# Second half of the residual in a hybrid decoder trunk: its sums of squares and its rows made on VectorE and ScalarE instead of by transposes on TensorE

## The chip, the cores and the metric

The kernel runs on one core of one Trainium2 chip. The metric is the device time of one execution in microseconds (us). Lower is better.

## The reference

The reference is one layer of a decoder trunk over 1024 tokens with 1024 channels, all in 32-bit floats. The part around the change is the end of the mixing half and the start of the MLP half:

```python
        m = jax.nn.sigmoid(sa) * y_a + jax.nn.sigmoid(sb) * y_b
        x = x + jnp.einsum("bsd,de->bse", m, w_o[l])      # out projection, residual

        h = rms_norm(x, g_mlp[l])                         # needs the sum of squares of each token
        f = jnp.square(jax.nn.relu(jnp.einsum("bsd,df->bsf", h, w_1[l])))   # up projection, 1024 -> 4096
        x = x + jnp.einsum("bsf,fd->bsd", f, w_2[l])      # down projection, residual
    return rms_norm(x, g_final)
```

`rms_norm` divides each token by the root of the mean of its squares over the channels.

## The kernel before

Every matrix product is done in 32-bit precision from three passes of a reduced form of it: an operand is split into a high part (`...h`) and a low part (`...l`), and the passes are high·high, high·low and low·high. The right operands are split by ScalarE (ACT, high part, L1386) and VectorE (DVE, low part, L1236). Most left operands (weights) are split by two ACT instructions (L65, L67) and one DMA issued from GpSimd (POOL, L66). On top of this, each product of 2 x 2 blocks is done in seven block products instead of eight (a Strassen-Winograd scheme), so sums and differences of blocks stand on DVE: `s1`, `s2`, `s3`, `s4` of the weights (L1695 to L1700) and `gt2` and the like of the tokens.

The order of the instructions on each engine is written out by hand. The lists `gseq` (gate and out projections, and the first two products of the up projection) and `useq` (the rest of the up projection) give the TensorE steps. A step is 12 matmuls of 128x512 on the four operand chunks; the third of each three uses the low part of the weight, the second the low part of the tokens, so the second matmul of a step is the first that needs the low part of the token operand's first half, and the eighth matmul the first that needs the low part of its second half. The tables `GX` and `UX` say what else is done beside each step: `up_load` (a 512 KB weight load from SP), `up_lhs` (the weights' sums and splits), `g_parts` (splits of a token operand), `g_t` (differences of token blocks). A running clock per engine (`clk`, `at`, `later`, `vector_work`) decides between which steps a deferred DVE instruction falls.

The residual `x1[kk, o, c2]` lies with channels on the partitions; `o` is the token half. It is wanted in two forms: normalized, as the token operand of the up projection (`x1_normed`, 8 DVE instructions a half, L482, from `x1`, a vector and the broadcast `rbm` of the reciprocal roots), and as rows of tokens in DRAM (`x1d`), from which the last residual sum reads it much later.

The first half (`o = 0`) takes its sums of squares by ACT squares (`x1_sq`, L1545), DVE adds (`x1_add`) and a column sum of 4 small matmuls (`x1_cols`, tile `cs`, L1574); its rows are turned by 8 DVE transposes (`x1_turn`) and written by 16 DMAs of 128 KB (`x1_rows_out`, L1568). The second half (`o = 1`) goes through `x1_rows`: 32 transposes on TensorE (tile `tr`, L1587), 8 ACT squares that add up along the row as they go (L1592), 8 DVE copies (L1596) and 4 DMAs of 512 KB (L1600). From the sums `x1_root` makes the reciprocal root (tile `stm`), `x1_diag` a diagonal matrix of it (`rdm`, L1627), and `x1_spread` the broadcast (`rbm`, L1637, on TensorE).

The TensorE steps around the change, in order: `go0e` to `go3e` (the last four of the out projection), `gu0a` (first of the up projection, start 905.98 us), the 32 transposes, `gu1a`, `gu2a`, `rbm`, `gu3a`, then `gu0a` to `gu3a` with the second token block, then `f0b`, `f1b`, `f0c`, `f1c`, `f0d`, `f1d`, and so on. The token operand of `f0b` and `f1b` is `gu6h`/`gu6l`; that of the `f0d`, `f1d` steps first `gu7h`/`gu7l` and in their second pass `gu4h`/`gu4l`.

The tiles come from pools. A tile waits until whoever used its slot last is done with it. `T(...)` draws from the pool `acts` (37 slots of 128x1024), which holds residual blocks, raw weights, split operands and rows. Which slot a new `T` gets therefore depends on the whole order of the `T` calls before it. `S(n)` in `up_lhs` draws from a pool of 5 slots for `s1` to `s4`; the first five are taken by `s1`, `s2` of weight pair 0, `s1`, `s2` of pair 1 and `s4` of pair 0, and `s3` of pair 0 is the sixth. Below, `o0_6` is the split of `s2` of pair 0, `o0_4` the split of a block of raw weight `w_1_raw`, and `o2_6` that of `s2` of pair 2, which is made from raw weights `w_4_raw` and `w_5_raw`.

Of the kernel before, what the change touches and what calls it, by code (L numbers as in the profile page):

```python
# [24 lines left out]
EPS = 1e-6  # L25
# [5 lines left out]
def trunk_kernel(ctx: ExitStack, tc: tile.TileContext, x, xt_in, xt_eo, vecs, w_in, w_a_out, w_b_pl, w_b_sq,  # L31
                 w_rg, w_o, w_1, w_2, g_final, out):

    nc = tc.nc
    cp = ctx.enter_context(tc.tile_pool(name="consts", bufs=1))
# [8 lines left out]
    def T(name, dt=F32, shape=(P, S)):  # L44
        return tp.tile(list(shape), dt, tag="T", name=name)
# [8 lines left out]
    HALVES = (slice(0, HS), slice(HS, S))  # L54
# [52 lines left out]
    ident = cp.tile([P, P], F32, name="ident")  # L107
# [371 lines left out]
    def dve(cost, ready, f, *a):  # L479

        fill(ready)
        f(*a)  # L482
        return at("V", cost, ready)
# [441 lines left out]
    def EV(name):  # L925
        return vp.tile([P, HS], F32, tag="ev", name=name)
# [113 lines left out]
    with tc.manual_schedule(engines=ENGINES):  # L1040
# [64 lines left out]
        def bank(name):  # L1105
            return zp.tile([P, HS], F32, tag="z", name=name)
# [430 lines left out]
    rst, rbk = {}, {}  # L1537
# [2 lines left out]

    sqs = []

    def x1_sq(i, m_):
        s = EV(f"sq{i}{m_}")
        nc.scalar.activation(s, x1[i // 2, 0, i % 2][:, HALVES[m_]], AF.Square)  # L1545
        sqs.append((at("A", 0.62, clk["V"]), s))

    def x1_add(n=1):
# [1 line left out]
            ready, s = sqs.pop(1)  # L1550
            later(ready, 0.63, tt, sqs[0][1], sqs[0][1], s, ALU.add)

    def x1_turn(kk):
        for th in range(2):
            r = T(f"x1r{kk}{th}")
            for c2 in range(2):
                src = x1[kk, 0, c2].rearrange("p (m h b j) -> p h m b j", m=2, h=2, j=32)[:, th]
                dst = r.rearrange("p (b m j) -> p m b j", m=4, j=32)[:, 2 * c2:2 * c2 + 2]
                dve(0.65, 0, nc.vector.transpose, dst, src)
            turned.append((kk, th, r))  # L1560

    turned = []

    def x1_rows_out():
        kk, th, r = turned.pop(0)
# [9 lines left out]
                             start=True, stop=True)  # L1575
        at("P", 0.9)

    def x1_rows(*ts):
        for t in ts:
            o, n = divmod(t, 4)  # L1580
            if n == 0:
                rst[o] = cp.tile([P, 6, 4], F32, tag="st6", name=f"stm{o}", bufs=2)
            rows = T(f"x1r{t}")
            for kk in range(2):
                ps = bank(f"tr{t}{kk}")
                for c in range(4):
                    nc.tensor.transpose(ps[:, c * P:(c + 1) * P],  # L1587
                                        x1[kk, o, c // 2][:, c % 2 * HS + n * P:c % 2 * HS + (n + 1) * P],
                                        ident)
                at("P", 0.45)  # L1590
                a = T(f"sq{t}{kk}")[:, 0:HS]
                nc.scalar.activation(a, ps, AF.Square, accum_out=rst[o][:, kk, n:n + 1])  # L1592
                at("A", 0.63, clk["P"])

                def copy(rows, kk, ps, t):
                    nc.vector.tensor_copy(  # L1596
                        rows[:, HALVES[kk]].rearrange("p (g c j) -> p c g j", g=4, c=4),
                        ps.rearrange("p (c g j) -> p c g j", g=4, c=4))
                    if kk:
                        nc.sync.dma_start(x1d[t], rows)  # L1600

                later(clk["P"], 0.63, copy, rows, kk, ps, t)
            if t == 7:
                x1_root(1)
            if o:
                vector_work(clk["V"])

    def x1_root(o):

        if o == 0:  # L1610
            rst[o] = cp.tile([P, 6, 4], F32, tag="st6", name=f"stm{o}", bufs=2)
        a, b, v, s = (rst[o][:, i, :] for i in range(4))
        if o:
            tt(v, a, b, ALU.add)
        nc.vector.tensor_scalar(v, v if o else sqs[1][:, 0:4], 1.0 / D, EPS, ALU.mult, ALU.add)
        nc.scalar.activation(s, v, AF.Sqrt)
        at("A", 1.5)

# [23 lines left out]
    def x1_normed(kk, o):  # L1642
        for c2 in range(2):
            hq[kk, o, c2] = src = a = x1[kk, o, c2]
            for i in range(2):
                c = 4 * kk + 2 * c2 + i
                dve(0.68, 0, nc.vector.scalar_tensor_tensor, a[:, HALVES[i]], src[:, HALVES[i]],
                    gmlp_c[:, c:c + 1], rbk[o], ALU.mult, ALU.mult)
# [136 lines left out]
    def g_get(n, f):  # L1785
# [57 lines left out]
    with tc.manual_schedule(engines=ENGINES):  # L1843
        for n, step in enumerate(bseq[2:], 2):
            taps["paused"] = False
            clk["A"], clk["V"] = max(clk["A"], clk["P"] + 0.5), max(clk["V"], clk["P"] - 2)
            b_post(*bseq[n - 1])
            b_mm(*step)
            for f, *a in BX.get(step, ()):
                f(*a)  # L1850
            vector_work(clk["P"] - 0.3)
        b_post(*bseq[-1])
        for n in range(len(gseq) + 1):
            clk["A"], clk["V"] = max(clk["A"], clk["P"] + 0.5), max(clk["V"], clk["P"] - 2)
            g_get(n - 1, g_post)
            if n == o0 + 22:
                x1_root(0)
            if n > o0:
                vector_work(clk["V"])
                if n == u0:  # L1860
                    to_mlp()
            g_get(n + 3, g_gate)
            g_get(n, g_mm)
            g_get(n + 4, g_lhs)
            g_get(n + 5, g_sums)
            for f, *a in GX.get(n, ()):
                f(*a)
            vector_work(clk["P"] - 0.3)
# [428 lines left out]
```

## Time and profile before

| | |
|---|---|
| time, median of 3 runs | 1528.98 us (1528.98 to 1529.56) |
| the profiled execution's own time | 1529.02 us |
| its span in the trace | 1527.2 us |
| mean granted TensorE clock | 0.998 |
| TensorE busy | 1517.7 us (99%) |
| VectorE busy | 1200.8 us (79%) |
| ScalarE busy | 927.0 us (61%) |
| GpSimd busy | 192.3 us (13%) |

The span runs from the first to the last instruction; the time has 1.8 us around it. In the lines of the profile a start and a duration are in us; a row "x4" is four instructions that follow each other; "[3.37 <-PE f0c]" is idle time before the row and what ended it. Neighbouring rows overlap a little, so the pitch of instructions (from start to start) is shorter than the duration of one.

### The profile page before, as it was taken

What the parts mean: (1) busy time and instruction counts of PE and PEld (TensorE: products, weight loads), DVE (VectorE), ACT (ScalarE), POOL (GpSimd) and SP (SyncE); (2) the same over time, 40 slices, a digit from 0 to 9 for tenths busy, and PEclk for the clock granted to TensorE, in tenths of its full rate; (3) what the DMA queues carried; (4) which work ended last, traced back from release to release, by engine and by line L of the source; (5) the groups of instructions that cost most, each with busy time, mean ns of one, the idle gap of its engine ahead of it and who ended that gap; (6) DMA issues with size and microseconds to landing.
All of it is one profiled execution on the core that took longest, in us unless ns stands there. A gap on an engine that the chain in (4) does not pass through costs nothing.

```text
span 1527.2 us, 18954 instructions
## 1 busy us (share of the span) xinstructions
PE 1517.7 (99%) x6712; PEld 1249.8 (82%) x6712; DVE 1200.8 (79%) x1640; ACT 927.0 (61%) x1299; POOL 192.3 (13%) x228
## 2 busy tenths in 40 slices
PE   9999999999999999999999999999999999999998
PEld 7878887888888888888888888888888888888886
DVE  7899996999999997788869879755555387777777
ACT  6749688586566657645575777554444455545475
POOL 0111011022222222000022322000000000101010
PEclk9999999999999999999999999999999999999999
DMA  9756778698997789863779897333333974776465
GB/s 352 187 145 159 176 177 191 193 260 213 266 260 173 186 207 273 292 231 121 263 205 302 186 200 189 124 126 111 111 111 111 307 261 129 187 201 167 110 123 153
DMA packets 130943, 295.48 MB, mean 193 GB/s; under 512 B 12912, under 2 KB 34928, under 8 KB 130848
## 3 DMA queue, kind: packets, MB, share of 16 engines
q1 hardware_dynamic: 98816, 214.60, 41.1%
q0 software_dynamic: 31600, 79.15, 28.2%
q8 instruction: 52, 0.85, 0.2%
q10 hardware_dynamic: 432, 0.53, 0.1%
q14 instruction: 43, 0.35, 0.1%
HBM read 148.74 MB, written 60.82 MB: 137 GB/s over the span
## 4 chain that ended last, share of the span: by engine, by line
PE 98%; DMA 1%; DVE 0%; issue 0%; SPq 0%; ACT 0%; DVEq 0%
PE z L745 16%; PE d1b L2017 2%; PE d2b L2017 2%; PE d0b L2017 2%; PE d3b L2017 2%; PE d0e L2017 1%; PE d0a L2017 1%; PE d3e L2017 1%; PE d3a L2017 1%; PE d1e L2017 1%; PE d1a L2017 1%; PE d2e L2017 1%; PE d2a L2017 1%; PE z L274 1%; PE rg L552 1%; PE rg L554 1%
## 5 line engine op out<-in xcount | busy, mean ns | idle before, releaser
L745 PE MATMUL z<-xh,win_h 128*128 128x512 f32 x368 | 115.5, 391 | 0.0
L745 PE MATMUL z<-xl,win_h 128*128 128x512 f32 x368 | 115.0, 390 | 0.0
L657 DVE SCALAR_TENSOR_TENSOR y<-u,vec,y 128x511 f32<-128x511 f32 (+14 forms) x120 | 88.2, 735 | 0.0
L745 PE MATMUL z<-xh,win_l 128*128 128x512 f32 x368 | 87.5, 390 | 0.0
L657 DVE SCALAR_TENSOR_TENSOR yt<-u,vec,yt 128x511 f32<-128x511 f32 (+6 forms) x112 | 82.4, 736 | 0.0
L657 DVE SCALAR_TENSOR_TENSOR y<-yt,csum,y 128x511 f32<-128x511 f32 (+6 forms) x112 | 82.4, 736 | 0.0
L745 PEld LDWEIGHTS z<-xh,win_h 128*128 128x128 f32 x368 | 69.1, 188 | 15.9 <-ACT win_h L67 0.5
L745 PEld LDWEIGHTS z<-xl,win_h 128*128 128x128 f32 x368 | 69.1, 188 | 14.9
L745 PEld LDWEIGHTS z<-xh,win_l 128*128 128x128 f32 x368 | 69.1, 188 | 14.6
L562 ACT ACTIVATE g<-rg,vec 96x1024 f32<-96x1024 f32 x32 | 35.5, 1110 | 72.9 <-PE rg L554 72.9
L1712 ACT ACTIVATE o<-s 128x512 fp32r<-128x512 f32 x56 | 33.7, 623 | 45.2 <-DVE s L1696 26.4
L66 POOL DMA_DIRECT2D zo<-zw x45 | 39.2, 871 | 134.7 <-ACT zo L65 116.8
L503 DVE SCALAR_TENSOR_TENSOR v<-xb,vec,v 128x1023 f32<-128x1023 f32 (+2 forms) x36 | 46.2, 1282 | 5.8 <-ACT v L494 4.9
L66 POOL DMA_DIRECT2D db_10l<-br x4 | 3.5, 876 | 338.3 <-DMA br<-in_w_dram 253.0
L66 POOL DMA_DIRECT2D win_l<-win_raw x23 | 20.0, 868 | 194.2 <-ACT win_l L65 159.4
L65 ACT ACTIVATE zo<-zw 128x512 fp32r<-128x512 f32 x45 | 28.2, 626 | 24.2 <-PE z2f L946 2.1
L1236 DVE TENSOR_TENSOR o<-s,o 128x512 fp32r<-128x512 f32 x56 | 37.3, 683 | 1.5 <-ACT o L1712 1.5
L66 POOL DMA_DIRECT2D zo<-zs x30 | 26.4, 879 | 74.9 <-ACT zo L65 62.8
L67 ACT ACTIVATE zo<-zw 128x512 fp32r<-128x512 f32 x45 | 27.9, 621 | 0.0
L598 DVE TENSOR_TENSOR_SCAN g<-a,g 128x1024 f32<-128x1024 f32 x12 | 27.5, 2291 | 0.4
L66 POOL DMA_DIRECT2D ga<-gsa x8 | 7.0, 874 | 161.0 <-DMA m<-mbd 150.8
L1236 DVE TENSOR_TENSOR o<-w_raw,o 128x512 fp32r<-128x512 f32 x38 | 25.9, 683 | 0.0
(3178 smaller groups left out, 4910.1 us busy)
## 6 DMA issues: line engine op xcount, KB each, us to landing
w_raw<-in_w_dram SPq DMA_DIRECT2D x32, 512.0 KB, 5.1
br<-in_w_dram SPq DMA_DIRECT2D x32, 512.0 KB, 5.8
ar<-fd SPq DMA_DIRECT2D x32, 512.0 KB, 6.6
zw<-in_w_in_dram SPq DMA_DIRECT2D x28, 512.0 KB, 6.9
win_raw<-in_w_in_dram SPq DMA_DIRECT2D x23, 512.0 KB, 4.6
win_l<-win_raw POOLq DMA_DIRECT2D x23, 512.0 KB, 4.8
zo<-zw POOLq DMA_DIRECT2D x45, 256.0 KB, 5.8
gates<-zg SPq DMA_DIRECT2D x32, 256.0 KB, 4.4
```

Source lines behind the costliest of these rows:

```text
L65: nc.scalar.activation(l, src, AF.Copy, scale=-1.0)
L66: nc.gpsimd.dma_start(l, src, accum_op=ALU.add)
L67: nc.scalar.activation(h, src, AF.Copy)
L274: nc.tensor.matmul(z0[i][:, HALVES[hf]], w0[i][w][:, k, :], xpart(a, hf, k), start=k == 0 and which == "hh", stop=k == 7 and which == ("hl ...
L503: nc.vector.scalar_tensor_tensor(v[:, d:S], a[:, 0:S - d], cbw_c[:, w * 12 + t:w * 12 + t + 1], v[:, d:S], ALU.mult, ALU.add)
L562: nc.scalar.activation(a, gps.pop((n, gi))[:HD, :], AF.Sigmoid, bias=(ba_c, bx_c)[gi][:, n:n + 1])
L598: nc.vector.tensor_tensor_scan(i, a, i, 0.0, ALU.mult, ALU.add)
L657: nc.vector.scalar_tensor_tensor(o[:, k:], a[:, 0:HS - k], c, o[:, k:], ALU.mult, add)
L745: nc.tensor.matmul(zps[s][:, HALVES[hf]], w[:, k, :], xw[k][part][hf], start=n == 0, stop=n == 23)
L1236: tt(l, src, h.bitcast(F32), ALU.subtract)
L1712: nc.scalar.activation(o[:, 0], src, AF.Copy)
L2017: nc.tensor.matmul(o, a, b, start=start and n == 0, stop=stop and n == len(todo) - 1, skip_group_check=not start or not stop)
```

## The change

The second half goes the first half's way. Eight ACT squares and seven DVE adds are put among the last steps of the out projection (`o0+24` to `u0+0`), the column sum of 4 small matmuls stands where the transposes stood, behind `gu0a`, and `x1_root(1)` is called one step later, at `u0+1`. `up_lhs(0, 6)` moves from `u0+0` to `u0+1`. `x1_normed` of the second half writes four new `T` tiles (`hq`) instead of overwriting `x1`, because the rows are now turned later, by 8 DVE transposes in the `useq` steps 12 to 18 and written by 16 DMAs of 128 KB in the steps 14 to 20. The 16 row DMAs of the first half move up from the `useq` steps 8 to 14 of the table to stand right behind their transposes. `x1_rows` is gone.

```diff
-    def x1_sq(i, m_):
-        s = EV(f"sq{i}{m_}")
-        nc.scalar.activation(s, x1[i // 2, 0, i % 2][:, HALVES[m_]], AF.Square)
+    def x1_sq(i, m_, o=0):
+        if o and (i, m_) == (0, 1):
+            sqs.clear()
+        name = f"sq{i}{m_}{o}"
+        s = T(name)[:, 0:HS] if o and (i, m_) in ((0, 1), (3, 0)) else EV(name)
+        nc.scalar.activation(s, x1[i // 2, o, i % 2][:, HALVES[m_]], AF.Square)
         sqs.append((at("A", 0.62, clk["V"]), s))
...
-    def x1_turn(kk):
-        for th in range(2):
-            r = T(f"x1r{kk}{th}")
...
     turned = []
+
+    def x1_turn(kk, th, o):
+        r = T(f"x1r{kk}{th}{o}")
+        for c2 in range(2):
+            src = x1[kk, o, c2].rearrange("p (m h b j) -> p h m b j", m=2, h=2, j=32)[:, th]
+            dst = r.rearrange("p (b m j) -> p m b j", m=4, j=32)[:, 2 * c2:2 * c2 + 2]
+            dve(0.65, 0, nc.vector.transpose, dst, src)
+        turned.append((kk, 2 * o + th, r))
...
-    def x1_rows(*ts):
...
     def x1_root(o):
 
-        if o == 0:
-            rst[o] = cp.tile([P, 6, 4], F32, tag="st6", name=f"stm{o}", bufs=2)
-        a, b, v, s = (rst[o][:, i, :] for i in range(4))
-        if o:
-            tt(v, a, b, ALU.add)
-        nc.vector.tensor_scalar(v, v if o else sqs[1][:, 0:4], 1.0 / D, EPS, ALU.mult, ALU.add)
+        rst[o] = cp.tile([P, 6, 4], F32, tag="st6", name=f"stm{o}", bufs=2)
+        v, s = rst[o][:, 2, :], rst[o][:, 3, :]
+        nc.vector.tensor_scalar(v, sqs[1][:, 0:4], 1.0 / D, EPS, ALU.mult, ALU.add)
...
             hq[kk, o, c2] = src = a = x1[kk, o, c2]
+            if o:
+                hq[kk, o, c2] = a = T(f"hq{kk}{c2}")
...
-        20: ((x1_add,), (x1_sq, 3, 1), (flush,), (x1_turn, 0)),
-        21: ((x1_add,), (flush,), (x1_cols,), (x1_turn, 1), (up_load, 0, (1,))),
+        20: ((x1_add,), (x1_sq, 3, 1), (flush,), (x1_turn, 0, 0, 0), (x1_turn, 0, 1, 0),
+             (x1_rows_out,), (x1_rows_out,)),
+        21: ((x1_add,), (flush,), (x1_cols,), (x1_turn, 1, 0, 0), (x1_turn, 1, 1, 0),
+             (x1_rows_out,), (x1_rows_out,), (up_load, 0, (1,))),
         22: ((x1_diag, 0), (up_load, 1, (1,))),
-        23: ((x1_spread, 0), (x1_normed, 0, 0)), 24: ((g_parts, "u", 1, 0), (g_parts, "u", 1, 1)),
-        25: ((x1_normed, 1, 0),), 26: ((g_parts, "u", 2, 0),), 27: ((g_parts, "u", 2, 1),)}.items()})
+        23: ((x1_spread, 0), (x1_normed, 0, 0)), 24: ((g_parts, "u", 1, 0), (g_parts, "u", 1, 1), (x1_sq, 0, 1, 1)),
+        25: ((x1_sq, 1, 1, 1), (x1_sq, 2, 1, 1), (x1_add, 2), (x1_normed, 1, 0), (x1_sq, 3, 1, 1)),
+        26: ((x1_add,), (x1_sq, 0, 0, 1), (x1_add,), (g_parts, "u", 2, 0), (x1_sq, 1, 0, 1)),
+        27: ((x1_add,), (x1_sq, 2, 0, 1), (x1_add,))}.items()})
     u0 = 2 * o0
     GX.update({u0 + n: v for n, v in {
-        0: ((up_lhs, 0, 6), (x1_rows, 4, 5, 6, 7)),
-        1: ((x1_diag, 1),), 2: ((x1_spread, 1), (up_lhs, 1, 6)),
+        0: ((x1_sq, 3, 0, 1), (x1_add,), (flush,), (g_parts, "u", 2, 1), (x1_cols,)),
+        1: ((x1_diag, 1), (up_lhs, 0, 6)), 2: ((x1_spread, 1), (up_lhs, 1, 6)),
...
+            elif n == u0 + 1:
+                x1_root(1)
...
-    UX.update({n: ((x1_rows_out,),) for n in range(8, 16, 2)})
+    UX.update({n: UX.get(n, ()) + ((x1_turn, n // 2 % 2, n // 4 - 3, 1),) for n in (12, 14, 16, 18)})
+    UX.update({n: UX.get(n, ()) + ((x1_rows_out,),) for n in (14, 16, 18, 20)})
```

What this does to the order is seen on three engines. On TensorE, behind the step `gu0a`, before the change:

```order
L1442 MATMUL gu0a<-gu1h_7703,gu_1_7696 128x512
L1587 MATMUL tr_7810<-ident,x_7587 128x128 x2
L1587 MATMUL tr_7810<-ident,x_7620 128x128 x2
L1587 MATMUL tr_7817<-ident,x_7654 128x128 x2
L1587 MATMUL tr_7817<-ident,x_7682 128x128 x2
```

Twelve such rows follow up to the step `gu1a`. After the change, at the same place (in the changed kernel L1576 is the column sum):

```order
L1442 MATMUL gu0a<-gu1l_7720,gu_1_7712 128x512
L1442 MATMUL gu0a<-gu1h_7719,gu_1_7712 128x512
L1576 MATMUL cs<-ones,sq_7722 128x1 x4
L1442 MATMUL gu1a<-gu1h_7716,gu_1_7739 128x512
L1442 MATMUL gu1a<-gu1l_7717,gu_1_7739 128x512
```

The column sum reads `sq_7722`, which the last of the seven adds on VectorE completes. On VectorE, from the diagonal `rdm` of the second half to the first split of the token operand `gu6`, before the change (L1695, L1696, L1698 and L1700 make `s1`, `s2`, `s4` and `s3`; the name's first number is the weight pair; the eight L482 rows with `rbm` are `x1_normed`):

```order
L1627 TENSOR_SCALAR rdm_7908<-ident,stm_7808 128x128 x2
L1695 TENSOR_TENSOR s_1_7937<-w_3_raw 128x512
L1696 TENSOR_TENSOR s_1_7938<-s_1_7937,w_2_raw 128x512
L482 SCALAR_TENSOR_TENSOR x_7587<-x_7587,vec,rbm_7932 128x512 x2
L482 SCALAR_TENSOR_TENSOR x_7620<-x_7620,vec,rbm_7932 128x512 x2
L482 SCALAR_TENSOR_TENSOR x_7654<-x_7654,vec,rbm_7932 128x512 x2
L482 SCALAR_TENSOR_TENSOR x_7682<-x_7682,vec,rbm_7932 128x512 x2
L482 TENSOR_TENSOR x_7141<-x_7587,x_7141 128x1024
L482 TENSOR_TENSOR x_7143<-x_7620,x_7143 128x1024
L482 TENSOR_TENSOR gt2u_7988<-x_7654,x_7141 128x1024
L482 TENSOR_TENSOR gt2u_7989<-x_7682,x_7143 128x1024
L1698 TENSOR_TENSOR s_0_8073<-w_0_raw,s_0_7801 128x512
```

After it (L1666, L1667, L1669 and L1671 are the same four):

```order
L1596 TENSOR_SCALAR rdm_7871<-ident,stm_7846 128x128 x2
L1666 TENSOR_TENSOR s_0_7876<-w_1_raw 128x512
L1667 TENSOR_TENSOR s_0_7877<-s_0_7876,w_0_raw 128x512
L1666 TENSOR_TENSOR s_1_7908<-w_3_raw 128x512
L1667 TENSOR_TENSOR s_1_7909<-s_1_7908,w_2_raw 128x512
L1669 TENSOR_TENSOR s_0_8048<-w_0_raw,s_0_7877 128x512
L1671 TENSOR_TENSOR s_0_8050<-w_0_raw,w_1_raw 128x512
L482 SCALAR_TENSOR_TENSOR hq_7935<-x_7595,vec,rbm_7903 128x512 x2
```

The sums of weight pair 0 stood ahead of `rdm` (`s1`, `s2`) and behind the `gt2u` rows (`s4`, `s3`); all four now stand between `rdm` and `x1_normed`. On SP, which issues the loads, the load of `w_5_raw` keeps its place behind the four `fd` stores of the first up projection steps; what it waits for is another. Before:

```order
L1501 DMA fd<-f_2_8040 128x512 [waits DMAHW6_49,Activation_49]
L1501 DMA fd<-f_3_8066 128x512 [waits DMAHW7_49,Activation_49]
L1679 DMA w_5_raw<-in_w_dram 128x1024 [waits DMASW2_49,DMAHW0_49,DMASW1_49,DVE_49]
L1679 DMA w_7_raw<-in_w_dram 128x1024 [waits DMASW6_49,DMAHW1_49,DVE_49,PE_49]
L1781 DMA fd<-fa_8152 128x512 [waits DMAHW2_49,Activation_49]
```

After:

```order
L1501 DMA fd<-f_2_8015 128x512 [waits DMAHW2_49,Activation_49]
L1501 DMA fd<-f_3_8041 128x512 [waits DMAHW3_49,Activation_49]
L1650 DMA w_5_raw<-in_w_dram 128x1024 [waits DMAHW4_49,DMASW7_49,DMAHW6_49,DVE_49,Activation_49]
L1650 DMA w_7_raw<-in_w_dram 128x1024 [waits DMAHW5_49,DVE_49]
L1752 DMA fd<-fa_8127 128x512 [waits Activation_49]
```

Before, the slot of `w_5_raw` was that of a residual block, whose last reader was the DVE instruction that makes `gu7l`. After, it is the slot of `w_1_raw`, whose last readers are the DVE instruction `s_0_8050`, the ACT instructions of the split `o0_4`, and that split's DMA, issued from POOL (the `DMASW7` in the row).

More of the change, by code (lines that the diff above doesn't have):

```diff
@@ L1551, in x1_add @@
             later(ready, 0.63, tt, sqs[0][1], sqs[0][1], s, ALU.add)
-    def x1_turn(kk):
-        for th in range(2):
-            r = T(f"x1r{kk}{th}")
[L1556 to L1560, printed above, removed]
-    turned = []
+    turned = []
+    def x1_turn(kk, th, o):
[5 more added lines that the diff above has]
+        turned.append((kk, 2 * o + th, r))
     def x1_rows_out():
@@ L1576, in x1_cols @@
         at("P", 0.9)
-    def x1_rows(*ts):
-        for t in ts:
-            o, n = divmod(t, 4)
-            if n == 0:
-                rst[o] = cp.tile([P, 6, 4], F32, tag="st6", name=f"stm{o}", bufs=2)
[L1583 to L1604, printed above, removed]
-            if o:
-                vector_work(clk["V"])
-    def x1_root(o):
-        if o == 0:
-            rst[o] = cp.tile([P, 6, 4], F32, tag="st6", name=f"stm{o}", bufs=2)
-        a, b, v, s = (rst[o][:, i, :] for i in range(4))
-        if o:
-            tt(v, a, b, ALU.add)
-        nc.vector.tensor_scalar(v, v if o else sqs[1][:, 0:4], 1.0 / D, EPS, ALU.mult, ALU.add)
+    def x1_root(o):
+        rst[o] = cp.tile([P, 6, 4], F32, tag="st6", name=f"stm{o}", bufs=2)
+        v, s = rst[o][:, 2, :], rst[o][:, 3, :]
+        nc.vector.tensor_scalar(v, sqs[1][:, 0:4], 1.0 / D, EPS, ALU.mult, ALU.add)
         nc.scalar.activation(s, v, AF.Sqrt)
```

## The prediction

> **What bounds the kernel now.** I read three views of the profile: first the chain of waits, for the engine that sets the end; then the timelines of TensorE, VectorE, ScalarE and GpSimd between 880 and 960 us, where the change lies; then the landings of the DMAs, in windows cut so narrow that they hold one issue. The chain of the whole execution:
>
> ```profile
> PE 98%; DMA 1%; DVE 0%; issue 0%; SPq 0%; ACT 0%; DVEq 0%
> ```
>
> TensorE is the bound in every stage: a microsecond taken from its queue is a microsecond gained, as long as what it needs next is there. So I look at TensorE's queue, and then at when its operands are ready. The timeline of TensorE at the transposes:
>
> ```profile
> 908.70 3.65 PE L1587 MATMUL tr<-ident,x 128*128 128x128 f32 x32
> 912.11 0.48 PE L1442 MATMUL gu1a<-gu1h,gu 128*128 128x512 f32 x1
> ```
>
> The 32 transposes hold the queue for 912.11 − 908.70 = 3.41 us. That is all the change can take off TensorE.
>
> **The change: the column sum in place of the transposes.** Four small matmuls come in. The first half's are in the timeline, eight records for four matmuls:
>
> ```profile
> 887.80 0.95 PE L1574 MATMUL cs<-ones,sq 128*128 128x1 f32 x8
> 888.61 0.49 PE L1442 MATMUL go2e<-go5h,go 128*128 128x512 f32 x1
> ```
>
> They cost 888.61 − 887.80 = 0.81. If their input were ready at 908.70, TensorE would gain 3.41 − 0.81 = 2.6. It is not. The input is complete after seven adds on VectorE, which stand between the last sums of the residual. VectorE's rows of that stretch, and four of the first half's transposes:
>
> ```profile
> 904.02 0.68 DVE L482 TENSOR_TENSOR x<-xe,go1e 128x512 f32<-128x512 f32 x1
> 906.18 0.69 DVE L482 TENSOR_TENSOR x<-xe,go3e 128x512 f32<-128x512 f32 x1 [0.88 <-PE go3e L1442]
> 906.78 0.68 DVE L1695 TENSOR_TENSOR s<-w_raw 128x512 f32<-128x512 f32 x1
> 907.50 0.69 DVE L1696 TENSOR_TENSOR s<-s,w_raw 128x512 f32<-128x512 f32 x1
> 883.76 2.49 DVE L482 STREAM_TRANSPOSE x1r<-x 128x512 f32<-128x512 f32 x4
> ```
>
> Two independent instructions start 0.60 apart (906.18, 906.78), a dependent one 0.72 behind its source (906.78, 907.50). From 904.02 the order is now add, add, `go1e`, add, add, `go2e`, add, add, `go3e`, with the second add of each pair dependent: 904.02 + 3 × 0.72 + 5 × 0.60 = 909.18 for the residual sum from `go3e`, 3.0 later than the row of before. It ends 0.69 later, at 909.87. Then its square runs on ScalarE. ScalarE's rows, with the square of the first half and what follows the square in the new order (a split of `gu2`, the copy `u<-gu0a`, the root):
>
> ```profile
> 880.97 0.63 ACT L1545 ACTIVATE sq<-x 128x512 f32<-128x512 f32 x1 [1.46 <-DVE x L482]
> 881.51 0.62 ACT L65 ACTIVATE go<-wo 128x512 fp32r<-128x512 f32 x1
> 905.84 1.05 ACT L65 ACTIVATE gu2l<-x 128x1024 fp32r<-128x1024 f32 x1
> 906.79 1.04 ACT L67 ACTIVATE gu2h<-x 128x1024 fp32r<-128x1024 f32 x1
> 914.95 0.21 ACT L1616 ACTIVATE stm<-stm 128x4 f32<-128x4 f32 x1 [0.43 <-DVE stm L1615]
> 915.06 0.58 ACT L1496 ACTIVATE u<-gu0a 128x512 f32<-128x512 f32 x1
> ```
>
> The square ends at 909.90 + 0.63 = 910.53, the last add, at the 0.69 of its neighbours, at 910.56 + 0.69 = 911.25, the column sum starts about 911.3 and `gu1a` at 911.3 + 0.81 = 912.1, against 912.11. TensorE stands idle for 2.6 of the 3.41 us: the gain is given back where it is made. Bounds: −2.6 if the sum were there in time, and about +0.2 if the square waits. Its tile takes the slot of the last turned rows of the first half, whose DMAs SP issues in this row:
>
> ```profile
> 889.64 13.48 SPq L1568 DMA_DIRECT2D x1d<-x1r  x12
> x1d<-x1r SPq DMA_DIRECT2D x1, 128.0 KB, 8.1
> w_raw<-in_w_dram SPq DMA_DIRECT2D x1, 512.0 KB, 7.9
> ```
>
> Twelve issues take 13.48, so the last is out at about 902; with 8.1, the landing of the first of them, it is in by 910.1, 0.2 behind 909.9. The loads `w_1_raw` and `w_3_raw` now queue behind all sixteen. With the slowest load of before, 7.9, they land at about 911, and are wanted after 914.5: covered.
>
> **The sums of the weights in front of the normalization.** Now `s1`, `s2`, `s4`, `s3` of pair 0 stand between `rdm` and `x1_normed`. `s3` takes the slot of `s2`, so it waits until the split `o0_6` of `s2` is over, down to the landing of its DMA. In the old order that DMA had gone out 19 us ahead of `s3`. VectorE, ScalarE and GpSimd in the old order:
>
> ```profile
> 916.03 0.17 DVE L98 RECIPROCAL stm<-stm 128x4 f32<-128x4 f32 x1
> 917.43 0.68 DVE L1695 TENSOR_TENSOR s<-w_raw 128x512 f32<-128x512 f32 x1
> 918.76 5.35 DVE L482 SCALAR_TENSOR_TENSOR x<-x,vec,rbm 128x512 f32<-128x512 f32 x8
> 908.77 0.62 ACT L65 ACTIVATE o<-s 128x512 fp32r<-128x512 f32 x1
> 909.68 0.87 POOL L66 DMA_DIRECT2D o<-s  x1 [0.17 <-issue]
> ```
>
> Now the sum. Behind the square come the two halves of the `gu2` split (906.79 − 905.84 = 0.95 each) and the copy (0.58): the square's start 909.90 + 0.54 + 0.95 + 0.95 + 0.58 = 912.92 for the root, done at 913.13. From the reciprocal to the first `s` it is 917.43 − 916.03 = 1.40: `s1` at 913.16 + 1.40 = 914.56, `s2` ends 0.72 + 0.69 later at 915.97. ScalarE's first split instruction ends at 916.0 + 0.62, GpSimd issues 909.68 − 908.77 − 0.62 = 0.29 later, at 916.9. The landings of 256 KB in the windows of one issue, at 899.96, 909.68 and 935.61:
>
> ```profile
> gu<-w_raw POOLq DMA_DIRECT2D x1, 256.0 KB, 5.1
> o<-s POOLq DMA_DIRECT2D x1, 256.0 KB, 7.7
> o<-s POOLq DMA_DIRECT2D x1, 256.0 KB, 3.4
> ```
>
> I take 5.1: there the 128 KB row DMAs were going out, and the four 512 KB row DMAs of before, which stood beside the slow landings, are gone at this place. The ends 3.4 and 7.7 stay for the range. So `s3` starts at 922.0 and `x1_normed` 0.60 later at 922.6, where it started at 918.76: **+3.9** (+2.2 to +6.5). Queued behind the waiting `s3` on VectorE are `x1_normed`, the differences `gt2u` and every low part after them; who waits for those are ScalarE's splits and through them TensorE. ScalarE, VectorE and TensorE there:
>
> ```profile
> 927.55 1.06 ACT L1386 ACTIVATE gu6h<-gt2u 128x1024 fp32r<-128x1024 f32 x1 [2.09 <-DVE gt2u L482]
> 932.42 0.39 PE L1724 MATMUL f0b<-gu6l,o 128*128 128x512 f32 x1
> 953.08 1.23 DVE L1236 TENSOR_TENSOR gu4l<-x,gu4h 128x1024 fp32r<-128x1024 f32 x1 [0.97 <-ACT gu4h L1386]
> ```
>
> The first `gu6l` would end at 927.55 + 3.9 + 1.06 + 1.23 = 933.7, against 932.4 where the second matmul of `f0b` wants it: TensorE waits 1.3 there.
>
> The Trainium skill, page "DMA: Bandwidth & Descriptors", section "Anatomy of one DMA — SWDGE (gpsimd) path", fits one DMA as about 2.0 us and the bytes at 436 GB/s. By that (an estimate from that page) 256 KB land in 2.6 and 512 KB in 3.2, and the whole sum, with the loads below, would be about +1.1. The trace doesn't bear it out here: its quickest 256 KB row is 3.4.
>
> **The load of `w_5`.** It now takes the slot of `w_1_raw`, and so waits for the DMA of the split `o0_4`, which reads `w_1_raw`. Before, it was out at 941.42, before that split ran. The rows of the split, of the load, and of what needs it:
>
> ```profile
> 945.07 0.87 POOL L66 DMA_DIRECT2D o<-w_raw  x1 [1.26 <-ACT o L65]
> o<-s POOLq DMA_DIRECT2D x5, 256.0 KB, 4.6
> o<-w_raw POOLq DMA_DIRECT2D x1, 256.0 KB, 5.9
> 941.42 4.98 SPq L1679 DMA_DIRECT2D w_raw<-in_w_dram  x2
> w_raw<-in_w_dram SPq DMA_DIRECT2D x1, 512.0 KB, 4.3
> w_raw<-in_w_dram SPq DMA_DIRECT2D x32, 512.0 KB, 5.1
> 951.46 0.63 ACT L1712 ACTIVATE o<-s 128x512 fp32r<-128x512 f32 x1 [3.37 <-PE f0c L1724]
> 952.00 1.04 ACT L1386 ACTIVATE gu4h<-x 128x1024 fp32r<-128x1024 f32 x1
> 955.54 0.39 PE L1724 MATMUL f0d<-gu4l,o 128*128 128x512 f32 x1
> ```
>
> ScalarE has little idle time from 927 to 948, so the split moves with the rest: its DMA goes out at 945.07 + 3.9 = 949.0. I take 4.6, the median of five between 935 and 960, and not the 5.9 of this very DMA, since the loads that ran beside it now wait for it; ends 3.4 and 5.9. So `w_5` is issued at 953.6; with 4.3 (the same load before; high end 5.1) it lands at 957.9. Then `s1` and `s2` of pair 2 on VectorE (0.72 + 0.69, to 959.3), `o2_6` on ScalarE, which stands ahead of the second `gu4h` there (951.46 to 952.00, 0.54), `gu4h` (1.04, to 960.9), `gu4l` (1.23, to 962.2). The eighth matmul of `f0d` wants it, at 955.54 before: TensorE is then **6.7** late in all, the earlier waits included. This is the term that decides.
>
> **What else moves.** The second half's 8 transposes go into the `useq` steps 12 to 18: two rows of 2.49, and 16 DMAs of 128 KB. The busy time of the engines there, from the table by stretches (TensorE, its loads, VectorE, ScalarE, GpSimd, then clock and DMA share):
>
> ```profile
> 960.00:990.00 30.00, 30.00 (x135) 24.82 (x134) 21.36 (x34) 16.16 (x24) 0.00 (x0) 1.00 0.29 106
> ```
>
> VectorE has 8.6 of 30 us free and takes 5.0 more; the DMA engines are at 0.29. I cost it at nothing. Without that cover, a step with two transposes hands its evacuation over 1.2 us late. The 8 copies, 4 large DMAs and 8 squares that go out were beside TensorE's work; the squares and adds that come in are in the sum above.
>
> **The sum.** 0.0 (column sum) + 6.7 (both waits, nested) = +6.7 on the profiled execution's own 1529.02, which is within 0.04 of the median: **1535.7 us**. With all landings at the quick end 6.7 − 1.7 − 1.2 = +3.8, 1532.8; at the slow end 6.7 + 2.6 + 1.3 + 0.8 = +11.4, 1540.4. I take 0.2% (3.1 us) as what a measurement of this kernel can tell from no change.
>
> **The rivals.**
> - *TensorE keeps the gain.* The sum is complete at 908.70 and both slots come free in time: −2.6, 1526.4. For it: TensorE is the bound, and 3.41 us are really gone. Against it: the VectorE queue, which has seven adds more before `go3e`'s square. It decides only if VectorE is 2.6 us quicker than its own pitch. 0.07; half of this I count as faster by over 0.2%, should other stalls go as well.
> - *The waits are not felt.* The landings come so quickly that neither slot is late, and the column sum alone counts: 0.0, 1529.0. It needs every landing quicker than its quickest row, since those alone leave +3.8; the rows of 3.4 to 7.7 speak against it. 0.07. By the fit of the Trainium skill's page named above the time would come out near this case, at 1530.1 (an estimate from that page).
> - *Only the load is late.* `s3` gets a free slot after all, or ScalarE catches up. Then the split's DMA goes out at 945.07 and the same chain gives 945.07 + 4.6 + 4.3 + 1.41 + 0.54 + 1.04 + 1.23 and some 0.1 for handing over = 958.3, +2.8: 1531.8, at the edge of what can be told. 0.09, half of it slower.
> - *The turns are felt too.* The late start pushes VectorE's evacuations into the transposes; one or two steps late by 1.2: 1536.9 to 1538.1. Against it stand the 8.6 us free. 0.09.
>
> **The chances.** The forecast has 0.68. Slower: 0.68 + 0.09 + 0.04 = 0.81; same: 0.03 + 0.07 + 0.05 = 0.15; faster 0.04. The range runs from the third rival's 1531.8 to 1541.0, the slow end with half a microsecond of a late turn; outside lie the first two rivals and a little on either side.
>
> **What would show it.** Right: TensorE idle by 2 to 3 us behind `gu0a`, released by VectorE's last add; `x1_normed` starting near 922.6 behind an `s` row that waited for a DMA; `f0b` waiting for `gu6l`; `w_5` issued near 953 and TensorE waiting at `f0d` for `gu4l`. Wrong: `gu1a` near 909.5, or `w_5` issued before 945, or a wait at another place of more than 2 us.

## The result and the profile after

The changed kernel takes 1535.14 us in the median of six runs (1534.44 to 1536.08), the kernel before 1529.47 us in six beside it (1528.98 to 1530.11). The ratio is 1.0037, with the 95% interval 1.0027 to 1.0048: slower by 5.67 us. The profiled execution of the changed kernel is the slowest of its six, 1536.08 us against the 1529.02 of before, so its rows show 7.06 us: a little more than the median. Of these, 0.46 us were there long before the change (`gu0a` starts at 906.44 where it started at 905.98). That leaves 6.6 us to be found between 906 us and the end; the rows below show 6.93 of it lost by 967 us and nothing lost behind.

The chain of the whole execution, which was TensorE at 98%:

```profile
PE 94%; DVE 2%; ACT 2%; DMA 1%; issue 0%; SPq 0%; ACTq 0%; DVEq 0%
```

The end is now set, for some stretches, by VectorE and ScalarE. The waits of TensorE from 890 to 1010 us (there were none before; total, times, longest):

```profile
PE cs L1576 <- DVE sq L482: 2.7, 1, 2.7
PE f0d L1695 <- ACT gu4h L1386: 1.0, 1, 1.0
PE f0d L1695 <- DVE gu4l L1236: 0.8, 1, 0.8
PE f0d L1695 <- DVE gu7l L1236: 0.7, 1, 0.7
```

Their sum is 5.2 us, and 2.6 of the first wait stand where the transposes had been. The waits alone therefore don't make up 6.93. What is missing is in TensorE's timeline, behind the column sum:

```profile
906.44 0.39 PE L1442 MATMUL gu0a<-gu1h,gu 128*128 128x512 f32 x1
...
911.99 1.05 PE L1576 MATMUL cs<-ones,sq 128*128 128x1 f32 x8 [2.67 <-DVE sq L482]
912.90 0.48 PE L1442 MATMUL gu1a<-gu1h,gu 128*128 128x512 f32 x1
917.27 0.45 PE L1442 MATMUL gu2a<-gu1h,gu 128*128 128x512 f32 x1
```

and in the table by stretches, of before and of after (the column ahead of the DMA share is the granted clock):

```profile
914.00:917.00 3.00, 3.00 (x15) 2.47 (x14) 2.47 (x10) 2.25 (x6) 0.55 (x1) 1.00 1.09 264
```

```profile
914.00:917.00 3.00, 3.00 (x9) 2.33 (x8) 2.83 (x9) 1.85 (x5) 0.87 (x1) 0.50 1.01 188
```

Both times TensorE is "busy" for all 3.00 us, but with 9 records in place of 15: the granted clock is 0.50. `gu1a`, a step of 12 matmuls, takes 917.27 − 912.90 = 4.37 us; the same step before took 2.82 (it started at 912.11, and the next row is where it ended):

```profile
914.93 0.39 PE L1442 MATMUL gu2a<-gu1h,gu 128*128 128x512 f32 x1
```

So the idle time behind `gu0a` is paid for twice: once as the wait, which only used up what the transposes had freed, and again as **1.55 us** of half clock. VectorE, ScalarE, GpSimd and SP on the way to `w_5`, and three landings in windows of one issue (of `o0_6`, which `s3` waits for, of `o0_4`, which `w_5` waits for, and of `w_5`, whose 4.3 reads like the row of before):

```profile
921.94 0.69 DVE L1671 TENSOR_TENSOR s<-w_raw,w_raw 128x512 f32<-128x512 f32 x1 [3.48 <-ACT gu L67]
922.55 5.35 DVE L482 SCALAR_TENSOR_TENSOR hq<-x,vec,rbm 128x512 f32<-128x512 f32 x8
917.49 0.87 POOL L66 DMA_DIRECT2D o<-s  x1 [2.12 <-PE gu1a L1442]
o<-s POOLq DMA_DIRECT2D x1, 256.0 KB, 4.3
948.70 0.87 POOL L66 DMA_DIRECT2D o<-w_raw  x1 [1.25 <-ACT o L65]
o<-w_raw POOLq DMA_DIRECT2D x1, 256.0 KB, 3.5
952.37 1.08 SPq L1650 DMA_DIRECT2D w_raw<-in_w_dram  x2
956.79 0.69 DVE L1666 TENSOR_TENSOR s<-w_raw 128x512 f32<-128x512 f32 x1 [3.10 <-DMA w_raw<-in_w_dram]
959.90 1.23 DVE L1236 TENSOR_TENSOR gu4l<-x,gu4h 128x1024 fp32r<-128x1024 f32 x1 [0.97 <-ACT gu4h L1386]
```

The label of the first row has to be read with care. "ACT gu" is only what came last by the profile; it is `s3`, which waits for its slot: 917.49 + 4.3 = 921.8 is the landing of the split's DMA. TensorE at `f0b` and `f0d`, and the clock behind it:

```profile
934.81 0.39 PE L1695 MATMUL f0b<-gu6l,o 128*128 128x512 f32 x1
947.95 0.50 PE L1695 MATMUL f0d<-gu7l,o 128*128 128x512 f32 x1 [0.73 <-DVE gu7l L1236]
949.21 0.39 PE L1695 MATMUL f1d<-gu7h,o 128*128 128x512 f32 x1
951.93 0.39 PE L1695 MATMUL f0c<-gu3h,o 128*128 128x512 f32 x1
959.92 0.50 PE L1695 MATMUL f0d<-gu4h,o 128*128 128x512 f32 x1 [1.03 <-ACT gu4h L1386]
961.18 0.50 PE L1695 MATMUL f0d<-gu4l,o 128*128 128x512 f32 x1 [0.76 <-DVE gu4l L1236]
963.01 0.63 PE L1695 MATMUL f1d<-gu4h,o 128*128 128x512 f32 x1
966.78 0.39 PE L1695 MATMUL f2b<-gu6h,o 128*128 128x512 f32 x1
963.00:966.00 3.00, 3.00 (x10) 2.40 (x9) 3.00 (x6) 2.79 (x5) 0.00 (x0) 0.64 0.12 47
```

`f0b` does not wait for `gu6l`. `f0d` waits for `gu7l` and later, as forecast, for `gu4h` and `gu4l`; then the clock drops a second time. The 0.64 is a mean over 3 us: cut into windows of 1 us it is 0.50 from about 961.8 to 965.2. The pass of `f1d` at full clock takes 951.93 − 949.21 = 2.72, the one behind the waits 966.78 − 963.01 = 3.77: **1.05** more, and the end of `f0d` loses 0.57 in the same way (1.83 from 961.18 to 963.01, against 1.26 from 947.95 to 949.21, both behind a wait). Against the rows of before,

```profile
956.67 0.39 PE L1724 MATMUL f1d<-gu4h,o 128*128 128x512 f32 x1
959.39 0.39 PE L1724 MATMUL f2b<-gu6h,o 128*128 128x512 f32 x1
```

`f1d` is 963.01 − 956.67 − 0.46 = 5.88 late and `f2b` 966.78 − 959.39 − 0.46 = 6.93. Step by step the lateness is 0.33 at `gu1a`, 1.88 at `gu2a`, 2.96 at the first `f1d` (949.21 against 945.79), then these 5.88 and 6.93. From there to the end the steps keep this distance within 0.1.

### The profile page after: what moved, and what is told of

It is laid out like the page before. It is cut to its first block, busy times and chain, and to the rows that moved or that the text cites. A ratio compares the mean times of both kernels' runs of the same rounds, so it can differ in the third digit from the quotient of the medians.

```text
span 1534.3 us, 18931 instructions
## 1 busy us (share of the span) xinstructions
PE 1519.4 (99%) x6688; PEld 1248.3 (81%) x6688; DVE 1205.2 (79%) x1646; ACT 927.4 (60%) x1291; POOL 192.2 (13%) x228
## 4 chain that ended last, share of the span: by engine, by line
PE 94%; DVE 2%; ACT 2%; DMA 1%; issue 0%; SPq 0%; ACTq 0%; DVEq 0%
PE z L745 16%; PE d1b L1995 2%; PE d2b L1995 2%; PE d0b L1995 2%; PE d3b L1995 2%; PE d0e L1995 1%; PE d3e L1995 1%; PE d3a L1995 1%; PE d2e L1995 1%; PE d2a L1995 1%; PE d1e L1995 1%; PE d1a L1995 1%; PE d0a L1995 1%; PE z L274 1%; PE rg L552 1%; PE rg L554 1%
## 5 line engine op out<-in xcount | busy, mean ns | idle before, releaser
L1683 ACT ACTIVATE o<-w_raw 128x512 fp32r<-128x512 f32 x38 | 23.6, 621 | 6.4 <-DMA w_raw<-in_w_dram 6.4
```

Source lines behind the costliest of these rows:

```text
L1683: nc.scalar.activation(o[:, 0], src, AF.Copy)
```

## The experiments

Three theories stood against each other. *Slots*: the two waits for slots (`s3` and `w_5`) cost the time, as forecast. *Half clock*: TensorE's idle time costs it, through the clock. *Turns*: VectorE's transposes cost part of it. Each kernel is the changed one with a small edit. All were timed against the kernel before, whose median in the three groups was 1529.50, 1529.53 and 1529.46.

**A free slot for `s3`.** `M` is a pool beside `T`.

```diff
-            sv[i, n] = op.tile([P, HS], F32, tag="s", name=f"s{n}_{i}", bufs=5).rearrange(
+            t = M(f"s{n}_{i}")[:, 0:HS] if (i, n) == (0, 3) else op.tile([P, HS], F32, tag="s", name=f"s{n}_{i}", bufs=5)
+            sv[i, n] = t.rearrange(
```

> The changed kernel, but s3 of weight pair 0 takes a tile of another pool, so nothing on VectorE waits for the split of s2 any more. Theory (the two slot waits decide, one nested in the other on the chain of VectorE and ScalarE): x1_normed starts about 921.1 instead of 922.55, held by the broadcast rbm (start 920.08) alone; everything behind it, w_5 too, comes 1.4 us sooner: 1535.1 - 1.4 = 1533.7. Rival A (the two losses of TensorE behind gu0a, 2.7 idle and 1.5 at half clock, are the loss, and the slot waits are covered): 1535.1.

Measured: 1536.15 us (1533.60 to 1536.97), ratio 1.0041 [1.0028, 1.0053]. Nothing was won: the 1533.7 of the slot theory was missed. TensorE and VectorE in it:

```profile
911.61 1.87 PE L1576 MATMUL cs<-ones,sq 128*128 128x1 f32 x8 [2.67 <-DVE sq L482]
913.34 0.77 PE L1442 MATMUL gu1a<-gu1h,gu 128*128 128x512 f32 x1
918.36 0.39 PE L1442 MATMUL gu2a<-gu1h,gu 128*128 128x512 f32 x1
922.17 2.06 DVE L482 SCALAR_TENSOR_TENSOR hq<-x,vec,rbm 128x512 f32<-128x512 f32 x3 [3.48 <-PE rbm L1606]
```

The wait for the slot is gone, and `x1_normed` starts at 922.17 all the same: it now waits for `rbm`, a TensorE step behind `gu1a` and `gu2a`, and in this execution the half clock covers the column sum too (913.34 − 911.61 = 1.73 us, not 0.91) and nearly all of `gu1a` (918.36 − 913.34 = 5.02, not 4.37). The slot and the half clock are two late inputs of one instruction; to take away one of them shows the other.

**A free slot for `w_5`**, and **both**:

```diff
-            raw = T(f"w1_{ff}_raw")
+            raw = (M if ff == 5 else T)(f"w1_{ff}_raw")
```

> The changed kernel, but the raw weight w_5 takes a tile of another pool, so its load no longer waits for the split of w_1_raw. Theory: the load goes out near 941, TensorE's waits at f0d for gu4h and gu4l go (1.0 + 0.8 us, and the slow matmuls behind them), and what stays is the lateness of 3.42 at f1d less 0.46 that the profiled run had from its start: about 1529.5 + 3.0 = 1532.4. Rival A (TensorE's own losses are the loss): 1535.1. Rival B (the load waits for other things next, the split of s2 of pair 1 or the queue): between 1534 and 1535.

Measured: 1532.78 us (1532.58 to 1534.26), ratio 1.0023 [1.0014, 1.0032]: 2.36 less than the changed kernel. The waits for `gu4h` and `gu4l` are gone, and this is what TensorE still waits for:

```profile
PE cs L1576 <- DVE sq L482: 2.7, 1, 2.7
PE f0d L1695 <- DMA o<-s: 0.2, 1, 0.2
```

> Both edits together: neither slot wait. Theory: x1_normed at 921.1, gu7l in time for f0d, w_5 in time: only the losses of TensorE behind gu0a stay, 0.3 for the column sum and 1.6 at half clock: 1529.5 + 1.9 = 1531.4. Rival A: 1535.1. If the two waits simply added instead of nesting, the savings of the two single edits would add: 1535.1 - 1.4 - 2.7 = 1531.0.

Measured: 1532.69 us (1531.11 to 1533.55), ratio 1.0017 [1.0008, 1.0027]. One wait is left, the 2.7 for the column sum, and 3.2 us of the loss. Since those 2.7 us lie in the gap of the transposes, the slot theory by itself would leave next to nothing here. My 1531.4 was missed as well: it took the half clock at 1.6, as in the profile of the changed kernel. In the profiled execution of this one the clock stands at 0.50 for 6.8 us, to 918.0, instead of 3.4. `f0b` starts at 935.69 there and at 932.19 before the change; less the 0.27 that was there at `gu0a` already, TensorE is 3.2 late. So about all that is left arises behind `gu0a`. The theory of the slots holds for `w_5` and falls as the whole account.

**The column sum a step later**, behind `gu1a` in place of `gu0a`, and the root, diagonal and sums of weights with it:

```diff
-        0: ((x1_sq, 3, 0, 1), (x1_add,), (flush,), (g_parts, "u", 2, 1), (x1_cols,)),
-        1: ((x1_diag, 1), (up_lhs, 0, 6)), 2: ((x1_spread, 1), (up_lhs, 1, 6)),
+        0: ((x1_sq, 3, 0, 1), (x1_add,), (flush,), (g_parts, "u", 2, 1)),
+        1: ((x1_cols,),), 2: ((x1_diag, 1), (up_lhs, 0, 6), (x1_spread, 1), (up_lhs, 1, 6)),
...
-            elif n == u0 + 1:
+            elif n == u0 + 2:
```

> The changed kernel, but the column sum stands one TensorE step later, behind gu1a instead of gu0a. TensorE is then not idle behind gu0a. Theory: no idle, so no half clock either; gu2a starts at 912.7 instead of 917.27; s3 falls behind x1_normed in VectorE's order, x1_normed starts about 918.4, and the load of w_5 still waits for the split of w_1_raw, so f0d waits for gu4l until about 957.9 where 953.3 would do: 1529.5 + 1.9, with slow matmuls behind that wait up to +2.9: 1531.4 to 1532.4. Rival A (losses of TensorE behind gu0a add to the rest): 1535.1 - 2.7 - 0.3 - 1.5 - 0.4 = 1530.2.

Measured: 1532.53 us (1531.61 to 1534.40), ratio 1.0021 [1.0012, 1.0030]. The sum no longer waits; 0.8 us comes back at `rbm`, which now waits for the diagonal. VectorE's list puts `s3` behind `x1_normed` here, which starts at 919.53 instead of 922.55, and SP issues `w_5` about as much earlier:

```profile
916.41 1.13 PE L1606 MATMUL rbm<-rdm,ones 128*128 128x128 f32 x8 [0.82 <-DVE rdm L1596]
919.53 5.35 DVE L482 SCALAR_TENSOR_TENSOR hq<-x,vec,rbm 128x512 f32<-128x512 f32 x8
949.23 1.19 SPq L1650 DMA_DIRECT2D w_raw<-in_w_dram  x2
957.00:960.00 3.00, 2.24 (x6) 1.56 (x7) 3.00 (x5) 1.58 (x4) 0.00 (x0) 0.71 0.23 87
```

Everything down to `f0d` moves forward by some 3 us, TensorE too, so the waits there stay (0.9, 1.0 and 0.8), and the clock drops behind them (0.71 in the mean of these 3 us). Both forecasts were missed, the 1531.4 to 1532.4 of the theory by 0.1 and the 1530.2 of the other by 2.3. The load that waits for its slot is the larger part of what is left: the run below that frees it as well takes 1530.07.

**Is it the clock?** The gap behind `gu0a` is filled with 24 transposes of a constant into an unused bank, so that TensorE is busy while it waits; nothing needs their output.

```diff
+    def x1_fill():
+        ps = bank("fill")
+        for n in range(24):
+            nc.tensor.transpose(ps[:, n % 4 * P:(n % 4 + 1) * P], ident, ident)
...
-        0: ((x1_sq, 3, 0, 1), (x1_add,), (flush,), (g_parts, "u", 2, 1), (x1_cols,)),
+        0: ((x1_sq, 3, 0, 1), (x1_add,), (flush,), (g_parts, "u", 2, 1), (x1_fill,), (x1_cols,)),
```

> The changed kernel with 24 transposes of a constant added on TensorE between gu0a and the column sum, into a bank that nobody reads (extra work, nothing is left out). They take 24 x 0.107 = 2.6 us where TensorE was idle for 2.7. Theory: no idle, no half clock: gu1a to gu2a takes 2.8 us again instead of 4.4 to 5.0; the end does not move, since s3 still waits for the split of s2 until about 921.9 and w_5 for its slot: 1535.1 (1534.3 to 1535.8). Rival (the half clock simply adds to the rest): 1535.1 - 1.6 to 2.2 = 1532.9 to 1533.5.

Measured: 1533.49 us (1533.16 to 1534.25), ratio 1.0026 [1.0016, 1.0035]. The reading that TensorE's own loss is hidden behind the later waits said 1535.1 and falls, and the rival's 1532.9 to 1533.5 holds: work that nobody needs makes the kernel 1.65 us faster. TensorE, its clock, and VectorE:

```profile
908.86 2.78 PE L1583 MATMUL fill<-ident 128*128 128x128 f32 x24
...
912.67 0.48 PE L1442 MATMUL gu1a<-gu1h,gu 128*128 128x512 f32 x1
915.48 0.39 PE L1442 MATMUL gu2a<-gu1h,gu 128*128 128x512 f32 x1
914.00:917.00 3.00, 3.00 (x15) 2.49 (x14) 2.84 (x8) 1.85 (x5) 0.87 (x1) 1.00 1.02 193
920.63 0.69 DVE L1676 TENSOR_TENSOR s<-w_raw,w_raw 128x512 f32<-128x512 f32 x1 [2.47 <-DMA o<-s]
```

`gu1a` takes 915.48 − 912.67 = 2.81 again, at clock 1.00. Also the split's DMA landed 1.0 quicker in this execution than in that of the changed kernel (3.3 against 4.3), and `f0d` waited for `gu7l` and `gu4l` alone and kept its clock; a new wait of 0.4 came at `f2c`, for ScalarE. How much of the 1.65 belongs to the first half clock and how much to that landing, one profile of each cannot tell.

**The gap filled, and the slots freed**: the same with `s3` from `M`, and with both.

> The filling transposes, and s3 of pair 0 in a tile of another pool. Neither the slot of s3 nor the late broadcast holds x1_normed. Theory: in the run without the filling the broadcast, late by the half clock, took the place of the slot wait; with both gone x1_normed starts about 919.5, 3 us sooner than in the changed kernel, and the chain that ends in the load of w_5 comes 3 us sooner: 1535.1 - 3.0 = 1532.1 (1531.5 to 1532.9). If only w_5's slot counts and not when its chain starts: 1535.1.

Measured: 1532.16 us (1531.59 to 1532.61), ratio 1.0016 [1.0007, 1.0025]; the 1532.1 of the theory holds, and `x1_normed` starts at 919.50.

> The filling transposes and both slot edits. Theory: what is left is the column sum's lateness of 0.3 to 0.8 at gu1a: 1529.5 + 0.3 to 0.8 = 1529.8 to 1530.3. If the 2.4 us lost behind gu0a in the run with both slot edits were not the half clock but something else: 1532.7 as before.

Measured: 1529.97 us (1529.45 to 1530.59), ratio 1.0003 [0.9994, 1.0012]: as expected, and not to be told from the kernel before. The account in medians is then closed: filling the gap −1.65, the slot of `s3` −1.33, the slot of `w_5` −2.19, from 1535.14 to 1529.97, and 0.44 is left, which lies inside the interval. The terms depend on their order. With the gap idle, the slot of `s3` on top of that of `w_5` was worth 0.09 (1532.78 to 1532.69); with the gap filled and `w_5` still late, 1.33. Filling the gap was worth 1.65 as the first edit and 2.72 as the last (1532.69 to 1529.97), more than either slot.

**Do the turns cost?** Each of the second half's transposes is done twice (the second writes the same again):

```diff
-            dve(0.65, 0, nc.vector.transpose, dst, src)
+            for _ in range(1 + o):
+                dve(0.65, 0, nc.vector.transpose, dst, src)
```

> The changed kernel with each of the second half's 8 transposes on VectorE done twice (8 more of 0.6 to 0.7 us between 975 and 995; nothing is left out). Theory (the turns lie in free time of VectorE): 1535.1 (1534.4 to 1536.0). Rival (VectorE's work in the up projection is felt): each doubled pair delays an evacuation by 1.3, up to four times: 1536.4 to 1540.

Measured: 1538.21 us (1537.80 to 1539.35), ratio 1.0059 [1.0045, 1.0072]: 3.07 more. VectorE and the waits of TensorE:

```profile
974.27 2.79 DVE L482 STREAM_TRANSPOSE x1r<-x 128x512 f32<-128x512 f32 x4
977.78 0.47 PE L1696 MATMUL f2d<-gu4h,o 128*128 128x512 f32 x1 [1.64 <-DVE fa L1724]
990.11 0.47 PE L1696 MATMUL f3c<-gu3h,o 128*128 128x512 f32 x1 [1.21 <-DVE fa L1722]
```

My theory of ample cover said 1535.1 and falls; the rival's 1536.4 to 1540 holds. One pair of transposes in a step is hidden: the changed kernel has no wait of TensorE there. Two pairs (2.79 us) are not: the evacuation behind them reaches TensorE 1.6 and 1.2 us late, in two of the four steps. Leaving the turns out altogether was not tried.

**A version that keeps the gain?** The later column sum and the free slot of `w_5` together:

> The column sum one step later, behind gu1a, and w_5 in a tile of another pool. Theory: TensorE stays 1.2 us ahead of the kernel before until f0d, waits there 1.2 for gu7l as in the run without the tile edit, and then no more: 1529.5 + 0.3 = 1529.8 (1529.3 to 1530.5). If the gain of 2.7 us on TensorE could be kept behind gu0a: 1527.0.

Measured: 1530.07 us (1529.40 to 1530.69), ratio 1.0002 [0.9994, 1.0011]: in the range, but the wait at `f0d` is not for `gu7l`. TensorE is ahead of the kernel before until `f0d`, and there it stops. The row at `f0d`, and on the way to it the split `o0_7` of `s3`, its landing, and the load of `w_5`; behind them the same landing in the kernel before:

```profile
944.50 0.73 PE L1695 MATMUL f0d<-gu7h,o 128*128 128x512 f32 x2 [1.56 <-DMA o<-s]
937.94 0.87 POOL L66 DMA_DIRECT2D o<-s  x1 [0.65 <-ACT o L65]
o<-s POOLq DMA_DIRECT2D x1, 256.0 KB, 6.5
938.68 13.61 SPq L1650 DMA_DIRECT2D w_raw<-in_w_dram  x2
```

```profile
937.13 0.87 POOL L66 DMA_DIRECT2D o<-s  x1 [0.65 <-ACT o L65]
o<-s POOLq DMA_DIRECT2D x1, 256.0 KB, 4.0
```

The 512 KB load, now free to start, goes out 0.74 us behind the split's DMA, which then lands in 6.5 us; in the kernel before the load went out at 941.42, when that DMA had landed (937.13 + 4.0). Here 937.94 + 6.5 = 944.4 is what `f0d` waits for. The profiles of all twelve kernels with the changed order let this be compared. In four the load goes out 0.67 to 0.74 us behind that DMA (`w_5` free by itself, this kernel and the next two), and the DMA lands in 6.5 to 6.7. In two it goes out 2.0 and 2.5 behind (both slots free, without and with the filling), in six after the landing, and the DMA lands in 3.3 to 4.1. Two further orders, also with the free slot of `w_5`, have the root in the same step as the sum, and the sums of pair 1 later (at `u0+4`; in the second one at `u0+5`, ahead of the split of `gu6`):

```diff
+        1: ((x1_cols,), (x1_root, 1), (x1_diag, 1), (up_lhs, 0, 6)), 2: ((x1_spread, 1),),
...
+        4: ((g_t, "u", 0, 2), (g_t, "u", 1, 2), (up_lhs, 1, 6)), 5: ((g_parts, "u", 6, 0),),
```

> As the run with the column sum later and w_5 in another pool, but the root and the diagonal follow the column sum at once, and the sums of weight pair 1 come behind the first differences of the tokens. Theory: x1_normed starts about 917.2 instead of 919.6, but 1.3 of that goes to the weight sums that now stand ahead of gt2u; the wait at f0d falls from 1.9 to about 1: 1529.5 - 0.6 = 1528.9 (1528.0 to 1529.8). If the wait at f0d hangs on the split of s3 and not on x1_normed: 1530.0.

Measured: 1530.12 us (1529.68 to 1530.83), ratio 1.0005 [0.9996, 1.0014]. The 1528.9 was missed, and the other reading, 1530.0, holds: the wait at `f0d` for the split is 1.7.

> The same with the sums of weight pair 1 one step further back, behind gt2u. Theory: the chain to gu7l and to the split of s3 comes 1.3 sooner again and little of the wait at f0d is left: 1529.5 - 1.9 = 1527.6 (1526.8 to 1528.8), unless the split of s2 of pair 1 now comes late for f1b (wanted at about 932.6, expected about 932.9), which would cost up to 1: 1528.6.

Measured: 1531.28 us (1530.94 to 1531.53), ratio 1.0011 [1.0002, 1.0020]; a miss. The sums of pair 1 now stand close ahead of the low parts, and `f0b` waits as well (1.2 in two waits), beside 1.3 at `f0d` for the split:

```profile
931.82 0.50 PE L1695 MATMUL f0b<-gu6l,o 128*128 128x512 f32 x1 [0.76 <-DVE gu6l L1236]
```

No version was faster than the kernel before. All three lost at the next transfer or the next VectorE instruction what they had won on TensorE.

## Why the prediction was right, and where it was not

- **The column sum gives its gain back.** Right in the wait: TensorE idle for 2.67, against 2.6 of the forecast, and `gu1a` 0.33 later than before, against 0.0. Wrong in the price: the sum has 0.0 for this place and should have had the half clock. The prediction spoke of TensorE's queue and operands only, and its list of what would show it has no line on the clock.
- **`s3` and the normalization.** Right: `x1_normed` at 922.55, forecast 922.6 (from 918.76 that is +3.84, which the prediction carries on as +3.9). The landing taken as 5.1 was 4.3; the profiled execution is 0.46 late as a whole, so the step is 0.5 too long.
- **`f0b` waiting for `gu6l` by 1.3.** Wrong. `gu6l` was late as forecast, but the late column sum and the half clock had made TensorE 1.93 us late by then, which is more than 1.3 (the second matmul of `f0b` at 934.81, 932.42 before, less the 0.46). In its place came 0.7 at `f0d`, for `gu7l`.
- **`w_5` decides.** Right in the chain, too much said in the weight. Taking the wait away is worth 2.36 and, with all else mended, 2.19: less than half of the 5.67. With neither slot late the prediction would have +0.0, and 3.2 were left; filling the gap, worth 1.65 to 2.72, weighs as much. The chain was measured link by link: split out at 948.70 (forecast 949.0), `w_5` issued at 952.37 (953.6), `gu4l` over at 961.1 (962.2). The term mis-sized is the landing of `o0_4`, taken as 4.6, measured 3.5. The prediction said that the loads beside it would be gone, and still took the price of a row that had them. Its sentence that the trace's quickest 256 KB row is 3.4 doesn't hold either: an issue of GpSimd at 879.29 landed in 3.3, and a 256 KB store of SP, in the window of 937.1, in 2.6.
- **"Both waits, nested".** Half right. The waits do nest: in the account, `s3` is worth 0.09 or 1.33 by what else is late. But `6.7` was to be all, and behind `f0d` the second drop of the clock adds 0.57 and 1.05. In the profiled execution `gu4l` was 5.2 late where TensorE wanted it (961.18 − 955.54 − 0.46) instead of 6.7, and `f2b` was 6.93 late: a term too large by 1.5 and one that was missing nearly cancel. That the 1535.7 is so near to 1535.14 is in this part luck.
- **The turns at nothing.** Right in the result, weak in the reason. The prediction set 8.6 us free in a stretch of 30 against 5.0; the kernel with the doubled turns has twice that work and loses 3.07. What counts is the free time ahead of each evacuation, and the rival of late turns (1.2 a step) had the right mechanism with the load of the doubled kernel.
- **The rivals.** "TensorE keeps the gain" fell with the first wait. "The waits are not felt" fell too: without both slot waits the kernel is 2.45 faster. "Only the load is late" has its test in the filled kernel with `s3` free: 1532.16, against the 1531.8 that this rival gave. Its condition did not hold in the changed kernel, and the nearness is in part chance: in that profile TensorE was 1.7 late behind `f0d`, where the rival has 2.8, and lost another 1.1 around `f2c`, where it waited for ScalarE.

## What to carry to other kernels

Time taken off the bound engine is a gain only if its next operand is there; otherwise it becomes idle time, and idle time of TensorE may cost more than itself, so look at the granted clock behind every wait that a change creates. Before a tile is allocated in a new order, follow who held the slot it now gets, down to the landing of a DMA that reads it: here a slot cost 2.2 us through a load that came 45 us later. And when two late inputs meet in one instruction, take both away before calling either harmless.

## What the runs showed of the hardware

**A short wait halves the clock.** Behind 2.67 us of idle time TensorE ran at a granted clock of 0.50, and with the same gap filled it stayed at 1.00. In windows of half a microsecond the halved stretch is 3.4 us long in the changed kernel (913.9 to 917.3), and 6.8 in the four other profiles with the open gap: 911.2 to 918.0 with `s3` free, and as long with `w_5` free, with both free and with the turns doubled. The three drops at `f0d` (the changed kernel, `s3` free, and the sum later) are 3.4 long each. The Trainium skill, page "TensorE: Matmul & The Clock Gate", section "Part 1: The HAM clock gate (the "warmup" mystery)", has a gate that passes half or all of the clock and is decided over windows of about 3.4 us that run freely. The lengths, one or two such windows, agree with this. The spread fits it too, though no run shows the cause of it: 1533.60 to 1536.97 with `s3` free, 1531.59 to 1532.61 for the same kernel with the gap filled. The rule of the page's section "HAM oscillation — how this bites in real kernels", that gaps of over about 3.4 us are to be avoided, is too mild by these rows: 2.67 was enough. Single waits of 0.7 to 1.7 left the clock alone, as here behind the 1.74 us wait at `f0d` in the first of the two further orders:

```profile
945.00:948.00 3.00, 3.00 (x14) 2.46 (x15) 3.00 (x5) 3.00 (x6) 1.12 (x2) 1.00 1.13 204
```

while 1.03 and 0.76 close together, in the changed kernel, halved it. Close waits of 0.76 and 0.43 at `f0b` in the second further order did not.

**One load beside a split's DMA.** A 256 KB DMA issued from GpSimd landed in 4.0 us when the next 512 KB load came after its landing, and in 6.5 when that load was issued 0.74 us behind it. The landing was 6.5 to 6.7 in all four profiles with the load 0.67 to 0.74 behind, and 3.3 to 4.1 in the nine others.
